# A hybrid decoder layer on one core: the output projection with the model's columns on the partitions, and x turned by VectorE block transposes through DRAM

## The chip, the core and the metric

The kernel runs on one core of a Trainium2 chip. A core has a matrix engine (TensorE, "PE" in the profile; its weight loads are "PEld"), a vector engine (VectorE, "DVE"), an activation engine (ScalarE, "ACT"), a general engine (GpSimd, "POOL") and a queue engine (SyncE, "SP") that here issues nearly all transfers to the sixteen DMA engines. SBUF is the working memory with 128 partitions, PSUM the small memory with eight banks into which TensorE writes, DRAM the large memory. The metric is the device time of one execution in microseconds (us); the kernel before took 1115.33 us, the median of three runs from 1115.24 to 1115.93.

## What is computed

One decoder layer for 1024 tokens of width 1024 (D), all in float32. The part that the change concerns, cut from the reference:

```python
        out_lru = rms_norm(h_lru * jax.nn.gelu(y_lru), lru_norm_w[l])       # 512 channels
        out_gdn = (rms_norm(o, gdn_norm_w[l]) * jax.nn.silu(z)).reshape(B, S, GDN_WIDTH)  # 512 channels
        mix = jnp.concatenate([out_lru, out_gdn], axis=-1) @ w_out[l]
        x = x + g1 * mix

        h = rms_norm(x, norm_mlp_w[l]) * (1.0 + sc2) + sh2
        x = x + g2 * (jnp.square(jax.nn.relu(h @ w_up[l])) @ w_down[l])

    return rms_norm(x, final_norm_w)
```

Ahead of it stand a norm of x, an input projection of 1024 by 3080, a gated linear recurrence (the LRU group) and a chunked gated delta rule with four heads (the GDN group). `g1`, `sc2`, `sh2` and `g2` are vectors over the 1024 columns of the model, worked out from `c` and `w_mod`.

## The kernel before, in words

**Precision.** Every large product is made of three matmuls on float32r operands: each operand is split into a rounded part "h" and a remainder "l", and h·h, h·l and l·h are summed (`mm3`). So a 128x128 by 128x512 step is three TensorE instructions, and each split costs a ScalarE cast and a VectorE or GpSimd subtraction.

**Order of the work.** The body does not issue instructions in program order. A recorder notes each operation with what it depends on, and `emit` then issues them in the order of a list of numbers that is stored in the kernel as packed text (`_ORDER`); a second list (`_SLOTS`) says which buffer each tile gets. So matmuls of several stages are interleaved one by one on TensorE, and each engine, SP among them, works through its own part of that list in order. The recorder is one line of code, which is why nearly every instruction of the profile has the line L331; stages are told apart by the names of the tiles.

**Input stages.** x (tiles of 128 tokens by 1024 columns) is normed and turned by TensorE, and the input projection gives channels on partitions and tokens along the free dimension. `key`, `query`, `value` and `chain` make the GDN group (output tiles `zz`, stored to `cat_d`), `lru` makes the LRU group (stored to `lru_d`), and `msum` gathers the squares of the LRU channels for their norm. The block transpose helper `blocks` (a VectorE transpose of 32x32 blocks over a tile of 128x1024) and its DRAM round trip are already used for the keys and values.

**Output projection.** `catload` loads the two groups back (tiles `gcm`, `lcm`) and splits them for the halves of 512 tokens (`gch`, `gcl`, `lch`, `lcl`); `wout` loads a row block of `w_out`, multiplies it by the norm weight and by g1 (broadcast over the partitions), and splits it. `gemm_o` then makes 128 tokens by 512 columns in one PSUM bank: the activations are stationary, the weights moving, twelve matmuls. There are sixteen such groups for the GDN channels (tiles `wg`), each added by VectorE to the tile of x that was loaded from DRAM, and sixteen for the LRU channels (tiles `wl`), each multiplied by the reciprocal norm `rsl` of its token and added. The tokens stand on the partitions, so `rsl` is a scalar per partition, and g1 has to be in the weights.

**Second norm.** For each of the eight token tiles `norm2` squares x with a sum along the row (ScalarE), takes the power of minus one half on GpSimd (`rsqrt8`), scales the row, stores the tile of x to DRAM (`x1_d`), and turns the eight 128x128 blocks on TensorE (tiles `h2T`); ScalarE and VectorE apply the column's scale and shift while they move the blocks out of PSUM to `h2r`. Three of the four quarters of the result are split at once (`h2h`, `h2l`, in pieces of 128x256).

**MLP.** The up and down products use Strassen-like sums with seven products for two by two blocks; `sums2` makes the sums of the quarters, `up` consumes the products in the order 1, 2, 6, 5, 7, 4, 3 (tiles `upx`, `upy`, `upz`). Products 1 and 2 need only the first half of the tokens, product 6 needs the sums over both halves. Four of the sixteen column blocks can be begun with products 1 and 2 before the first sum is there. The down product (tiles `dn`) goes over seven products again, and during the second of them the tiles of x are loaded back from `x1_d` (tiles `xb`); then the gated result is added and the final norm is made (`final_early`, `final_late`, `final_parts`).

Of the kernel before, what the change touches and what calls it, by code (L numbers as in the profile page):

```python
# [106 lines left out]
def dram_box(ap):  # L107
# [8 lines left out]
    'c-obl2Xqxx_xAUhB!m!p$IwxF2~E0!2+~17M4E-B2nYyBQ;JCMVxft^OO=kIAc&wy?@d}H^e#O>GH3sPXObYk-}n93`qo{^ojZ5t%szWR``OPvGq<3mlKmPcMI<HfMZ'  # L116
    '}Y%T8zI^a!`xPF@2~JeD|jsc~Q1#4!O*qkxTlFw36|9N9)N}t;$~o*{N0J500xW+cb-$mNS}3Zfa&}DPL$;M%<*&bM`s@mzOU&Zcxa&gxy-6(H?Lm)w5bgzSbEsKwp<'
    '#nnF%%3)!waw33vPax#<eFX_87jjQ<Vb(VCJBYH{;NH|u9Vs9zQ%dxBVu9lE!IixXqQ1dZ<8o9@uvh#nhrj)93LI326XBnkAXP(s)l1~T8#~hPKu4{rG)mrkG=9O6eQ'
    '99^ttt(444OUw1qV1)Y?8c_QnVBb7bdJ8rjJN7@eDd{#wv}=En*7GG4dkKT(nZo*3(G$BBuq+UeY9ki&3Lu1Y+^R07_Y2E$rufhdYqqKGRQ=IReI`FiIkt2n<s9jX{4'
    '_#)>mY#=9l!$C>H;vkk&F)N6A;(NEWDS2R$gO_`WOAS<2^jI*XWglMnI1MIFhp&fc8(HH8ddv}ffpR<6~Lbt&_XlodqgfR@r%%@VG3j89vLZx*@1c{SyGb^fcwEY@jF'  # L120
    '@NipuOMk7;wQg%kyft4Zm_yb@zKle0y{j52g^0#d{8=0vgyDmV`k1X8+CKD~_+Mp^Wc5~>!U_90f45%Ktg;8|i_1@Z-s3g$*XT|C!WcPWQ%jVIwafHFbJ9k#{a8P@9Y'
    'D-Iouq^1nvT;CBrU!fCWG*41m65uK4Yu~(o*-DT{f!>*DvH2K3he!?tt<;cyzXw!}nilC6gO3G?f2ng^&=x1ekiPKS(bPm(em%$ID0fE+aEvMW$rOw$G)i?g&ZgXJP('
    'FiDLmG+E{B7xm(QnsJ<_~Lmxk$2@dN^7Wssc>+5K~O)C~3HqbZaWw{Tg@-bFjvTBfiFa5a2T>VCufq|V|d8GCrR`v1qN!{l4@#~TiS2QCLy9K&Z%M1DoqlHR09l)_;I'
    'o5a^{323Gx--jy(o9C_%b@aO8I705f`L(7M;Un#d*VRb0%^e~)rHu;T3RvZWgtpHX1KV&-DG15(5HNpQeM+2nM{V2_O|(zc(+6=mz>f(*p*VwGtbHzuRr6fBcQ7|OcH'
    '{v9#}ZQRZGjWdRit(TJ1>gcjo_oZKFpdH<nxn7bn!$4a~S3h<jNlNL~F&_Ud^oJEZsdt}54GDof-)cCfUQO!}LAFAa60-j-(C9hRsjzv>lY-A3Br*FW@;z9bc~;1BkH'
    'rW=S*W1T2(a^^%bGl6f%zzx&LzINU@zouN2)wUCJSf~fIttmksEwZ06_wkIp(l#^i>$_UTys5+W8{)M=Kf$~4T2E(7BfPyD9Hcirw6!cFHdW-2PSN^0N#>C=F9zI{QZ'
    'C32+XlaGx3Sv7c*LSIe%mZ3$kNd;-Ze?bD@;pz%k6Xew#g?CY^3*t9Rya}$b9`8&t}ti%wSz++Su#*7M%PU*Dj2$H*9(Nz^Hb^_YcX<N~RW;4w3FQlc^&u%?JJu-YOd'
# [12 lines left out]
    'I4V4|@hOm{QJ^Jar}8M@j=o57~OzsdU&HY=bj?PEB4ye_qez4a*AZ20aqQ&#%h_T~!pK9!W$Q|Q>&;WHbkg|yPr-{tktaWc*}Fn4v3U&k!91w&HHo`mIIDrxSo^kUF='  # L140
    'o~h!0?oHDI+6i|1TkEs`8S!)|UBnFgrin2<wYlHP3?gRXa>r|Dm)c_934ek|{qn<QwO8NI8M0Xm`{Nkph#v+rc9`mRBe^<WS6KyBZ<tO}+x~3E=|{5Ll(jG0T;6&AYp'
# [247 lines left out]
def hybrid_body(ctx, tc, x, c, norm_mix_w, norm_mlp_w, w_mod, b_mod, w_in,  # L389
# [837 lines left out]
    def lru(ct, st, yy):  # L1227
# [509 lines left out]
```

## Time and profile before

| | |
|---|---|
| median of three runs | 1115.33 us |
| the profiled execution's own time | 1115.21 us |
| its span, first to last instruction | 1113.4 us |
| TensorE busy | 1102.6 us (99%) |
| VectorE busy | 784.2 us (70%) |
| ScalarE busy | 614.6 us (55%) |
| GpSimd busy | 246.0 us (22%) |
| DMA traffic | 240.30 MB in 132520 packets |

The page gives for each engine the time in which it had an instruction in flight. TensorE's instructions overlap: one matmul of 512 columns is shown with about 0.39 us, but the next one starts some 0.23 us after it, so the share says that it always had something to do and not how fast. The groups of instructions are listed as engine, operation, the tile written and the tiles read, their shape, a count, the busy time and the mean time of one. The view of a stretch of time gives for each engine its busy time there and, in brackets, how many instructions it touched, then the granted TensorE clock, the DMA engines' share and the transfer rate.

### The profile page before, as it was taken

The page shows a single profiled execution, that of the slowest core. Times are in us where ns is not written, and L with a number is a line of the kernel's source. Part 1 is how long each engine was busy: PE and PEld are TensorE (multiplying, and loading weights), DVE is VectorE, ACT ScalarE, POOL GpSimd, SP SyncE. Part 2 cuts the span into 40 slices and gives each one's busy share as a digit, 9 for nine tenths or more (in the row PEclk, how much of TensorE's full clock was granted, in tenths as well). Part 3 has the DMA queues.
Part 4 walks back from the last instruction along what each step waited for, and adds up shares of the span by engine and source line. Part 5 has one row for each costly group of instructions (what it writes and reads, how often), then busy time and mean ns, then how long its engine had stood idle before and what let it go on. Part 6 is the DMA issues. An engine that isn't in the chain of part 4 may idle for free.

```text
span 1113.4 us, 16336 instructions
## 1 busy us (share of the span) xinstructions
PE 1102.6 (99%) x6186; PEld 920.5 (83%) x6186; DVE 784.2 (70%) x1119; ACT 614.6 (55%) x956; POOL 246.0 (22%) x159
## 2 busy tenths in 40 slices
PE   9999999999999999999999999999999999999997
PEld 8799888888887878788888888788888888888886
DVE  5779996878787774798666757767574576673564
ACT  6759454536388882876645545455555433442442
POOL 1000200110204324000113121222500466903130
PEclk9999999999999999999999999999999999999999
DMA  9837815566751741310787687678999866946312
GB/s 342 305 111 248 287 62 176 191 226 214 263 170 69 254 161 50 138 53 29 256 288 247 234 293 252 220 235 292 380 376 397 326 230 222 341 171 245 132 57 94
DMA packets 132520, 240.30 MB, mean 216 GB/s; under 512 B 11141, under 2 KB 55770, under 8 KB 132442
## 3 DMA queue, kind: packets, MB, share of 16 engines
q1 hardware_dynamic: 132202, 239.04, 61.4%
q8 instruction: 48, 0.79, 0.3%
q14 instruction: 30, 0.25, 0.1%
q10 hardware_dynamic: 240, 0.23, 0.1%
HBM read 178.38 MB, written 60.86 MB: 215 GB/s over the span
## 4 chain that ended last, share of the span: by engine, by line
PE 91%; ACT 5%; DVE 2%; issue 1%; POOL 0%; POOLq 0%; ACTq 0%
PE dn L331 28%; PE upx L331 16%; PE upz L331 8%; PE k_p L331 4%; PE wg L331 4%; PE upy L331 4%; PE wl L331 4%; PE ly_p L331 4%; PE v_p L331 3%; PE q_p L331 3%; PE lx_p L331 3%; PE ch L331 2%; PE z_p L331 2%; PE cho L331 1%; ACT L331 1%
## 5 line engine op out<-in xcount | busy, mean ns | idle before, releaser
L331 PE MATMUL upx<-h2h,U 128*128 128x512 f32 x512 | 164.9, 395 | 0.0
L331 PEld LDWEIGHTS upx<-h2h,U 128*128 128x128 f32 x512 | 96.1, 188 | 22.8 <-ACT ek L331 0.7
L331 DVE TENSOR_TENSOR U<-wu,U 128x512 fp32r<-128x512 f32 x112 | 82.0, 751 | 23.8 <-ACT U L331 22.9
L331 POOL TENSOR_TENSOR wd<-wd,wd 128x512 f32<-128x512 f32 x32 | 45.6, 1429 | 238.4 <-DMA wd<-in_w_down_dram 181.8
L331 PE MATMUL upx<-h2l,U 128*128 128x512 f32 x256 | 95.2, 396 | 0.0
L331 ACT ACTIVATE act<-act 128x512 f32<-128x512 f32 x112 | 68.9, 629 | 32.7 <-DVE act L331 31.4
L331 ACT CAST U<-wu 128x512 fp32r<-128x512 f32 x112 | 66.6, 616 | 36.6 <-DVE wu L331 24.0
L331 PE MATMUL upz<-h2h,U 128*128 128x512 f32 x256 | 86.6, 394 | 0.0
L331 PEld LDWEIGHTS upx<-h2l,U 128*128 128x128 f32 x256 | 48.1, 188 | 11.5 <-issue 0.4
L331 PEld LDWEIGHTS upz<-h2h,U 128*128 128x128 f32 x256 | 48.1, 188 | 11.4 <-DVE act L331 0.2
L331 ACT COPY ek<-upx 128x512 f32<-128x512 f32 x48 | 27.7, 584 | 52.9 <-PE upx L331 52.5
L331 DVE TENSOR_TENSOR act<-upz,ek 128x512 f32<-128x512 f32 x32 | 22.0, 688 | 39.2 <-PE upz L331 20.0
L331 PE MATMUL upz<-h2l,U 128*128 128x512 f32 x128 | 47.9, 395 | 0.0
L331 PE MATMUL upy<-h2h,U 128*128 128x512 f32 x128 | 44.3, 398 | 0.0
L331 ACT ACT_TABLE_LOAD x28 | 35.9, 1283 | 11.7 <-DVE z_b L331 5.4
L331 POOL TENSOR_TENSOR R<-R,R_5o 128x1024 f32<-128x1024 f32 x8 | 22.9, 2872 | 81.8 <-DMA R_5o<-in_w_down_dram 81.8
L331 DVE TENSOR_TENSOR wu<-wu,wu 128x512 f32<-128x512 f32 x48 | 35.1, 736 | 0.4 <-DMA wu<-in_w_up_dram 0.2
L331 ACT ACTIVATE vn<-ch,bcoef 128x128 f32<-128x128 f32 x32 | 11.7, 367 | 34.2 <-PE ch L331 34.0
L331 PE MATMUL v_p<-hh,v_wh 128*128 128x258 f32 (+2 forms) x96 | 29.5, 335 | 0.9 <-ACT z_st L331 0.9
L331 PE MATMUL ly_p<-hh,ly_wh 128*128 128x512 f32 (+2 forms) x96 | 29.6, 326 | 0.3 <-ACT ta L331 0.3
L331 PE MATMUL v_p<-hl,v_wh 128*128 128x256 f32 (+2 forms) x96 | 29.8, 338 | 0.0
L331 PE MATMUL v_p<-hh,v_wl 128*128 128x258 f32 (+2 forms) x96 | 29.4, 335 | 0.0
(567 smaller groups left out, 3411.7 us busy)
## 6 DMA issues: line engine op xcount, KB each, us to landing
L<-aod SPq DMA_DIRECT2D x56, 512.0 KB
R<-in_w_down_dram SPq DMA_DIRECT2D x40, 512.0 KB
wu<-in_w_up_dram SPq DMA_DIRECT2D x32, 512.0 KB
aod<-as SPq DMA_DIRECT2D x64, 256.0 KB
wd<-in_w_down_dram SPq DMA_DIRECT2D x32, 512.0 KB
aod<-act SPq DMA_DIRECT2D x48, 256.0 KB
x<-in_x_dram SPq DMA_DIRECT2D x16, 512.0 KB
sc_w<-in_w_mod_dram SPq DMA_DIRECT2D x16, 512.0 KB
```

Source lines behind the costliest of these rows:

```text
L331: op.fn(*[res(v) for v in op.a], **{n: res(v) for n, v in op.k.items()})
```

## The change

The output projection now has the model's columns on the partitions and 512 tokens along the free dimension: the weights are stationary, the activations moving. The number of matmuls of the projection and their size stay. What goes with it:

- x is needed in the turned layout. `turn_x` loads each of the eight tiles of x again during the input projection, transposes its 32x32 blocks on VectorE and stores it to DRAM (`xb_d`); `residual` reads the turned tiles (`xT`) with runs of 64 floats.
- g1 is a scalar per partition now (`mod_col` instead of a row that is broadcast through DRAM), applied in `gated` while the result leaves PSUM; the weights get only the norm weight.
- The LRU norm can't be applied as a scalar per partition any more. `rows8` sums over the partitions by matmuls with ones, VectorE turns the sums, GpSimd takes the power, and the row goes through DRAM (`ln_d`) and comes back broadcast over the partitions (`lrus_b`); `catload` multiplies the LRU tiles by it before they are split.
- Four of the sixteen groups (`MERGED`, the second half of the tokens) sum the GDN and LRU channels in one PSUM bank, and leave PSUM once.
- The second norm is made for each half of the tokens after its eight column groups: squares and sums over the groups, `rows8`, and four TensorE transposes that spread the row over the partitions (`n2b`). There is no turn of the data itself. Scale and shift go over tiles of 128x512.
- x for the end is turned back: `turn_back` loads, block-transposes and stores the eight tiles during the up product, and `xload` reads them in two pieces each with runs of 64 floats. The operations of the final norm read x through strided views.
- `_ORDER` and `_SLOTS` are replaced, for the whole kernel.

The diff without the packed lists, cut to its core:

```diff
+    def turn_x(t):
+        xr, hb = big(f"xe{t}"), big(f"xeb{t}")
+        SP.dma_start(out=xr, in_=xs[t])
+        blocks(hb, xr)
+        SP.dma_start(out=xb_d[t], in_=hb)
...
+        if 6 <= i < 14:
+            turn_x(i - 6)
         if i == 7:
-            mod_row(2, 0, "g1")
+            g1 = mod_col(2, "g1")
...
-    V.tensor_scalar(two(rsl), colsum(msum, "lrus"), 1.0 / 512, 1e-6, op0=ALU.mult, op1=ALU.add)
-    rsqrt8(rsl, rsl)
+    def rows8(acc, name, n, scale):
+        pr, rw = ps(name), big(f"{name}_w")
+        mms([(pr[32 * j:32 * j + 32, 0:n], ones[:, 0:32], acc[:, n * j:n * j + n], True, True) for j in range(4)])
+        V.transpose(rw[:, 0:n], pr[:, 0:n])
+        r = small(f"{name}_r", n // 32)
+        V.tensor_scalar(r, rw[:, 0:n:32], scale, 1e-6, op0=ALU.mult, op1=ALU.add)
+        rsqrt8(r, r)
+        return r, rw
+    rl_, rw_ = rows8(msum, "lrus", 256, 1.0 / 512)
+    V.transpose(rw_[:, 256:512], bc(rl_, 32))
+    SP.dma_start(out=ln_d.rearrange("a (j n) -> (a j) n", j=4), in_=rw_[0:P:32, 256:512])
+    rlb = big("lrus_b")
+    SP.dma_start(out=rlb, in_=ln_d[0:1, :].to_broadcast([P, T]))
...
-        V.scalar_tensor_tensor(out=wr, in0=wr, scalar=sc, in1=g1b, op0=ALU.mult, op1=ALU.mult)
-        A.copy(wh, wr)
-        (V if k % 2 else G).tensor_tensor(out=wl, in0=wr, in1=wh.bitcast(F32), op=ALU.subtract)
+        A.activation(wh, wr, AF.Identity, scale=sc)
+        V.scalar_tensor_tensor(out=wl, in0=wr, scalar=sc, in1=wh.bitcast(F32), op0=ALU.mult, op1=ALU.subtract)
...
+    def gemm_o(p, cats, ws, k, hf, start, stop):
+        for q in range(4):
+            c, d = cats[(hf, q // 2)], slice((q % 2) * 512, (q % 2) * 512 + 512)
+            mm3(p, tuple(w[:, k * P:(k + 1) * P] for w in ws[q]), tuple(x_[:, d] for x_ in c), start and q == 0, stop and q == 3)
+    MERGED = ((1, 4), (1, 5), (1, 6), (1, 7))
+            SP.dma_start(out=v3(xT[q, hf], 64),
+                         in_=xb_d[4 * hf:4 * hf + 4].rearrange("t (i c) (b x) -> (c b) (t i) x", c=32, b=4)[:, :, 64 * q:64 * q + 64])
+    def gated(p, k, o, r):
+        V.scalar_tensor_tensor(out=v3(o, 32), in0=v3(p, 32), scalar=g1[:, k:k + 1], in1=r, op0=ALU.mult, op1=ALU.add)
...
+    def finish(k, hf):
+        p, o = ps(f"wl{k}{hf}"), slot(X1, k, hf)
+        if (hf, k) in MERGED:
+            gemm_o(p, gcat, gw_, k, hf, True, False)
+            gemm_o(p, lcat, lw, k, hf, False, True)
+            gated(p, k, o, residual(k, hf))
+        else:
+            gemm_o(p, lcat, lw, k, hf, True, True)
+            gated(p, k, o, v3(o, 32))
+        if k == 0:
+            norms[hf] = big(f"n2a{hf}")[:, 0:512]
+            A.activation(norms[hf], o, AF.Square)
+        else:
+            sq = half(f"n2s{k}{hf}")
+            A.activation(sq, o, AF.Square)
+            V.tensor_tensor(out=norms[hf], in0=norms[hf], in1=sq, op=ALU.add)
+    def norm2(hf):
+        r, _ = rows8(norms[hf], f"n2_{hf}", 128, 1.0 / D)
+        pb = ps(f"n2b{hf}")
+        for b in range(4):
+            tr(pb[:, b * P:(b + 1) * P], r[:, b:b + 1].to_broadcast([P, P]), ident)
+        rb = big(f"n2r{hf}")[:, 0:512]
+        V.tensor_copy(rb.rearrange("p (j b n) -> p j b n", j=4, b=4), pb.rearrange("p (b j n) -> p j b n", b=4, j=4))
+        for k in range(8):
+            rv = raw2[(g, hf)][e][:, d]
+            V.scalar_tensor_tensor(out=rv, in0=slot(X1, k, hf), scalar=A2[:, k:k + 1], in1=rb, op0=ALU.mult, op1=ALU.mult)
+            A.activation(rv, rv, AF.Identity, bias=sh2[:, k:k + 1])
+            if (g, hf) in alone:
+                A.copy(av, rv)
+                V.tensor_tensor(out=bv, in0=rv, in1=av.bitcast(F32), op=ALU.subtract)
-        for g in range(2):
-            ph = ps(f"h2T{t}_{g}")
-            for j in range(4):
-                tr(ph[:, j * P:(j + 1) * P], h2[:, (g * 4 + j) * P:(g * 4 + j + 1) * P], ident)
...
+    def turn_back(n):
+        SP.dma_start(out=xr, in_=x1_d[n])
+        blocks(hb, xr)
+        SP.dma_start(out=x1b_d[g, hf, e], in_=hb)
...
+    def xload(n):
+        th, tp, i = n // 4, n // 2 % 2, n % 2
+        b = x1[th, tp, i] = big(f"xb{n}")
+        for k in range(2):
+            SP.dma_start(out=b.rearrange("p (k q x) -> p k q x", k=2, q=8)[:, k],
+                         in_=x1b_d[i, th].rearrange("e (i c) (b x) -> (c b) (e i) x", c=32, b=4)[:, :, 128 * k + 64 * tp:128 * k + 64 * tp + 64])
```

More of the change, by code (lines that the diff above doesn't have):

```diff
@@ L1311, in catload @@
             SP.dma_start(out=m, in_=d_[h])
+            if norm is not None:
+                V.tensor_tensor(out=m, in0=m, in1=norm, op=ALU.mult)
             for hf in range(2):
@@ L1327, in hybrid_body @@
     gcat = catload("gc", cat_d)
     gw_ = [wout(k) for k in range(4, 8)]
-    def gemm_o(cats, ws, t, i, name, then):
-        p = ps(name)
-        s = halves[i]
-        hf, tt = t // 4, t % 4
-        for k in range(4):
-            ts_ = slice((k % 2) * 512 + tt * P, (k % 2) * 512 + (tt + 1) * P)
-            a, w = cats[(hf, k // 2)], ws[k]
-            mm3(p, (a[0][:, ts_], a[1][:, ts_]), (w[0][:, s], w[1][:, s]), k == 0, k == 3)
-        then(p, s)
-    x1 = [big(f"x1_{t}") for t in range(NT)]
@@ new lines, in hybrid_body, with residual @@
+    MERGED = ((1, 4), (1, 5), (1, 6), (1, 7))
+    X1 = {(g, hf): [big(f"x1_{g}{hf}{e}") for e in range(2)] for hf in range(2) for g in range(2)}
+    slot = lambda b, k, hf: b[(k // 4, hf)][k % 2][:, (k % 4 // 2) * 512:(k % 4 // 2) * 512 + 512]
+    xT = {}
+    def residual(k, hf):
+        q = k // 2
+        if (q, hf) not in xT:
+            xT[q, hf] = big(f"xT{q}{hf}")
+            SP.dma_start(out=v3(xT[q, hf], 64),
+                         in_=xb_d[4 * hf:4 * hf + 4].rearrange("t (i c) (b x) -> (c b) (t i) x", c=32, b=4)[:, :, 64 * q:64 * q + 64])
+        return v3(xT[q, hf], 64)[:, :, 32 * (k % 2):32 * (k % 2) + 32]
@@ L1349, in hybrid_body @@
+    def gated(p, k, o, r):
+        V.scalar_tensor_tensor(out=v3(o, 32), in0=v3(p, 32), scalar=g1[:, k:k + 1], in1=r, op0=ALU.mult, op1=ALU.add)
+    for hf in range(2):
+        for k in range(8):
+            if (hf, k) not in MERGED:
+                p = ps(f"wg{k}{hf}")
+                gemm_o(p, gcat, gw_, k, hf, True, True)
+                gated(p, k, slot(X1, k, hf), residual(k, hf))
+    lcat = catload("lc", lru_d, rlb)
     lw = [wout(k) for k in range(4)]
@@ L1414, in sums2 @@
         yield
-    for t in range(NT):
-        for i in range(2):
-            gemm_o(lcat, lw, t, i, f"wl{t}{i}",
-                   lambda p, s: V.scalar_tensor_tensor(out=x1[t][:, s], in0=p, scalar=rsl[:, t:t + 1], in1=x1[t][:, s],
-                                                       op0=ALU.mult, op1=ALU.add))
-        if t == 0:
-            dump("x1", x1[0])
-        norm2(t)
+    for hf in range(2):
+        for k in range(8):
+            finish(k, hf)
+        norm2(hf)
     wu_r = w_up.rearrange("a (k p) n -> (a p) k n", p=P)
@@ L1554, in hybrid_body @@
         if m < 10:
+            turn_back(m - 2)
             g2_acc = g2_acc or big("g2_acc")
@@ L1657, in add_to @@
     def add_to(th, i, j, v_, e):
-        e.tensor_tensor(out=xt(th, i, j), in0=xt(th, i, j), in1=v_, op=ALU.add)
+        e.tensor_tensor(out=xt(th, i, j), in0=xt(th, i, j), in1=v3(v_, 32), op=ALU.add)
     banks = {}
@@ L1668, in hybrid_body @@
             if at == 2:
-                x1[d] = big(f"xb{d}")
-                SP.dma_start(out=x1[d], in_=x1_d[d])
+                xload(d)
                 if d == 3:
```

322 lines of the change are left out of this document (153 added, 169 removed).

## The prediction

> **What bounds the kernel now.** I read the engines' shares first, then what TensorE waited for, then stretches of time. The shares and the chain that ended last:
>
> ```profile
> PE 1102.6 (99%) x6186; PEld 920.5 (83%) x6186; DVE 784.2 (70%) x1119; ACT 614.6 (55%) x956; POOL 246.0 (22%) x159
> PE 91%; ACT 5%; DVE 2%; issue 1%; POOL 0%; POOLq 0%; ACTq 0%
> ```
>
> TensorE always has a matmul in flight, and the chain goes through it for 91% of the span. All that it waited for (total, times, longest):
>
> ```profile
> PE warm L331 <- DVE ones L331: 1.0, 1, 1.0
> PE v_p L331 <- ACT z_st L331: 0.9, 1, 0.9
> PE gate L457 <- ACT ly_st L331: 0.7, 2, 0.4
> PE iy L457 <- ACT ttc L331: 0.5, 1, 0.5
> PE ly_p L331 <- ACT ta L331: 0.3, 1, 0.3
> ```
>
> Some 3.4 us in 1113. So the time is the number of TensorE instructions times their spacing, and a change is worth what it takes from that count, less the waits that it brings. The spacing comes from two stretches of 56 us, the first with the second norm's transposes, the other with none:
>
> ```profile
> 439.00:495.00 56.00, 56.00 (x276) 44.51 (x275) 45.81 (x102) 38.92 (x85) 4.23 (x7) 1.00 0.25 95
> 560.00:616.00 56.00, 56.00 (x243) 45.36 (x242) 36.54 (x55) 29.92 (x54) 12.51 (x9) 1.00 0.79 268
> L331 PE MATMUL h2T<-ident,h x64: 269/272/275, 439.7 to 492.4; 128*128 128x128 f32 x64
> ```
>
> The second gives 56/243 = 0.2305 us for a matmul of 512 columns. The first holds all 64 transposes and 276 - 64 = 212 matmuls; these take 48.9 us, which leaves 7.1 us, or 0.111 us for a transpose, though each is shown with 272 ns. The granted clock is 1.00 in both.
>
> **TensorE, part by part.** The projection's matmuls keep their number and size (16 + 16 groups of twelve), so the exchange of operands costs nothing here. The 64 transposes go: -7.1 us. New are two sums over partitions and eight transposes that spread the row:
>
> ```profile
> L457 PE MATMUL lrus_r<-msum,ones x8: 379/392/404, 416.4 to 416.6; 128*32 128x256 f32 x8
> 415.00:424.00 9.00, 0.64 (x8) 0.16 (x8) 0.37 (x1) 1.00 0.69 236
> L331 PE MATMUL lrus_c<-ident,lrus_row x2: 271/272/274, 418.2 to 418.6; 128*128 128x128 f32 x2
> ```
>
> The LRU sum of 256 columns takes 0.64 us (the second row is that tile alone). With 128 columns it is between half of that and the whole; I take half, since the columns are what streams: 2 x 0.32 = 0.6 us, at most 1.3. The eight transposes are 8 x 0.111 = 0.9 us. The LRU norm loses its two transposes and g1 gains two: nothing. Sum: -7.1 + 0.6 + 0.9 = -5.6 us, with bounds of -4.9 and, if the new ones all fell into gaps, -7.1.
>
> **Hand-over of the LRU norm.** Before, `rsl` was applied after the matmuls. Now the LRU operands can't be split before the norm has gone through DRAM and back. The GDN norm of each head already goes this way, and its rows give the first pass in order:
>
> ```profile
> L457 PE MATMUL on<-nv,ones x32: 378/379/404, 207.8 to 335.9; 128*32 128x256 f32 x32
> L331 SPq DMA_DIRECT2D on_b<-ond x4: 319/330/372, 215.8 to 343.2; - x4
> L331 DVE TENSOR_TENSOR zz<-zz,on_b x4: 1216/1216/1908, 220.8 to 358.6; 128x1024 f32<-128x1024 f32 x4
> L331 ACT CAST gch<-gcm x8: 602/614/623, 297.1 to 382.6; 128x512 fp32r<-128x512 f32 x8
> 417.00:445.00 28.00, 17.34 (x57) 10.53 (x57) 4.84 (x7) 1.00 0.16 57
> ```
>
> From the first sum (207.8) to the product with the broadcast row (220.8) are 13.0 us, then 1.2 us of it and 0.6 us of cast: 14.8 us at most, since that product may have queued on VectorE; up to the issue of the load at 215.8 alone it is 8.0 us, so 9.8 us is a lower bound. The cover is the last row, the GDN groups alone: 57 of their matmuls stand after the LRU sum at 416.4, 57 x 0.2305 = 13.1 us that need no LRU operand. The exposure is between nothing and 1.7 us.
>
> **Hand-over of the second norm.** For the first half of the tokens, its chain lies under the second half's projection: 8 x 12 matmuls, 22.1 us. For the second half the cover is products 1 and 2 of the four column blocks begun, 4 x 24 matmuls, again 22.1 us. The chain:
>
> ```profile
> L331 DVE SCALAR_TENSOR_TENSOR x<-wl,rsl,x 128x512 f32<-128x512 f32 x16 | 12.0, 748 | 10.4 <-PE wl L331 10.1
> L331 ACT ACTIVATE act<-act 128x512 f32<-128x512 f32 x112 | 68.9, 629 | 32.7 <-DVE act L331 31.4
> L331 DVE TENSOR_TENSOR x<-wg,x 128x512 f32<-128x512 f32 x16 | 10.8, 689 | 8.0 <-PE wg L331 8.0
> L331 DVE STREAM_TRANSPOSE on_w<-on x4: 409/444/450, 210.0 to 336.4; 128x256 f32<-128x256 f32 x4
> L331 POOL TENSOR_TENSOR ssq<-ssq,mhalf 128x1 f32<-128x1 f32 x16 | 11.4, 717 | 73.6 <-DVE ssq L331 73.4
> L331 ACT COPY ek<-upx 128x512 f32<-128x512 f32 x48 | 27.7, 584 | 52.9 <-PE upx L331 52.5
> L331 DVE TENSOR_TENSOR h2r<-h2r,h2r 128x1024 f32<-128x1024 f32 x8 | 9.8, 1222 | 0.1
> L331 DVE TENSOR_TENSOR h2l<-h2r,h2h 128x1024 fp32r<-128x1024 f32 x8 | 9.5, 1221 | 0.1
> 480.00:502.00 22.00, 22.00 (x106) 17.68 (x105) 20.61 (x36) 15.79 (x32) 0.55 (x1) 1.00 0.06 25
> 502.00:524.00 22.00, 22.00 (x96) 17.88 (x96) 21.13 (x28) 14.30 (x25) 0.00 (x0) 1.00 0.03 13
> ```
>
> Gating 0.75, square 0.63, add 0.69, the sum on TensorE 0.64, the turn 0.44, the power 0.72, four transposes 0.6 (0.27 and three more at 0.111), the copy at 0.58: 5.1 us. Then VectorE alone: eight scalings at 0.75, the four sums ahead of product 6 at 1.22 and two splits at 1.22, 13.3 us. Together 18.4 us against 22.1 us. VectorE also has four additions of about 0.69 us for the begun blocks in that time, and its share is 94% and 96% in these two stretches already, so 0.9 us is left: just covered if the 96 matmuls are kept for it. On ScalarE the shifts wait for VectorE here, and behind them are queued the copies `ek` that free PSUM banks for TensorE.
>
> I set down 0.5 us for each of the three hand-overs, the mean of the five waits of TensorE after the start (2.4 us): +1.5 us. Their bounds are nothing and the prices of the rivals.
>
> **VectorE, ScalarE, GpSimd elsewhere.** Sixteen block transposes are added, eight in the input projection and eight in the up product:
>
> ```profile
> L331 DVE STREAM_TRANSPOSE nv<-v2T 128x1024 f32<-128x1024 f32 x1 | 2.1, 2059 | 0.9 <-ACT v2T L331 0.9
> 83.00:300.00 217.00, 215.41 (x1852) 193.18 (x1851) 181.38 (x292) 121.42 (x199) 23.50 (x14) 1.00 0.61 205
> 560.00:720.00 160.00, 160.00 (x696) 128.88 (x695) 104.82 (x151) 81.19 (x145) 33.68 (x24) 1.00 0.75 254
> ```
>
> Eight times 2.06 us is 16.5 us. In the first stretch VectorE goes from 181.4 to 197.9 of 217 us, in the second from 104.8 to 121.3 of 160 us; it stays under TensorE in both, so the cost is nothing, and without that cover 16.5 us each. The page "VectorE: DVE Perf Modes" of the Trainium skill, "Rules for kernel authors", speaks against this: it gives the turn of a 128x128 tile to TensorE and keeps the vector engine for 32x32 blocks. By the rows above both sides are right: 33 us of VectorE replace 7.1 us of TensorE, and the rule would decide if VectorE did. The rest of VectorE's and ScalarE's work (fewer and larger pieces in the norm, four products with the LRU row at 1.22 us) changes by a few us and lies under TensorE as now. The strided views of the final norm have no row; between 0 and, at worst, double for the last pieces of 0.4 to 0.7 us, some 2 us; I take 0, since the counts of elements stay.
>
> **Transfers.** `turn_x` and `turn_back` each add 8 MB; the DMA engines' shares of 0.61 and 0.75 leave room for the 22 us that 8 MB take at 384 GB/s. x in both directions comes in runs of 256 B now, for which there is no row. The nearest are runs of about 500 B and the busiest stretch of long ones:
>
> ```profile
> DMA packets 3033, 1.50 MB, mean 300 GB/s; under 512 B 163, under 2 KB 3028, under 8 KB 3032
> 48.00:53.00 5.00, 5.00 (x37) 4.49 (x36) 4.93 (x5) 1.44 (x3) 0.00 (x0) 1.00 1.06 300
> 779.00:863.00 84.00, 84.00 (x364) 68.05 (x363) 50.81 (x49) 44.24 (x54) 14.34 (x10) 1.00 1.02 384
> L331 SPq DMA_DIRECT2D xb<-x1d x8: 320/333/599, 816.7 to 851.2; - x8
> L331 POOL TENSOR_TENSOR xb<-xb,keep x8: 1284/1750/2269, 885.2 to 1031.0; 128x512 f32<-128x512 f32 x8
> ```
>
> A packet of some 500 B takes 5 x 16 x 1.06 / 3033 = 0.028 us of one engine. A tile of 512 KB in runs of 256 B has 2048 packets: 1.4 us if only the bytes count (384 GB/s), 3.6 us if a packet costs as much as one of 500 B. Eight tiles add 0 to 18 us of DMA time, for the residual in a stage with room, for `xload` in the stretch from 779 to 863 us, where the DMA engines are full. I take nothing for the path: the tiles are needed 34 us after the last load (851.2 to 885.2). The Trainium skill ("DMA: Bandwidth & Descriptors", Specifications) says that transfers under 512 B miss the line rate because of a read-modify-write; by that the price would be at the upper end or above it.
>
> **The sum.** The profiled execution took 1115.2 us (span 1113.4 and 1.8 us around it): 1115.2 - 5.6 + 1.5 = 1111.1 us. It lies 0.1 us under the median, so the forecast is 1111.2 us.
>
> **The rivals.**
> - *VectorE becomes the bound at the second norm's barrier; slower.* Place: between the last projection matmul and product 6. For it: VectorE is full there now, and the scalings of four tiles, spread so far, fall into one burst behind a reduction. Against it: the bare chain is 3.7 us shorter than the cover. If half of the 96 matmuls are spent earlier, 11.1 us of cover are left for 18.4 us of chain and 2.8 us of additions: 10.1 us of stall, and 1115.3 - 5.6 + 10.1 + 1.0 = 1120.8 us. It decides from a stall of 7.8 us on, when some 38 matmuls are gone.
> - *The LRU row comes late; no change.* If the LRU group's own chain slips by 3 us because VectorE is fuller, the exposure is 1.7 + 3 us: 1115.3 - 5.6 + 4.7 + 1.0 = 1115.4 us.
> - *Short runs fill the DMA engines.* 18 us more of transfers in a full stretch; with half of it exposed as waits for the second product's operands, 1111.2 + 9 = 1120.2 us. Against it: the order can spread these loads over the 34 us.
> - *The transposes go and nothing is exposed*, and the 2.4 us of waits go too with the new order: 1115.3 - 5.6 - 2.4 = 1107.3 us.
> - *The change does not do what it says*: TensorE keeps eight transposes for the norm, which are in the sum; the data's own are all gone by the diff, so this gets no chance of its own.
>
> **How the numbers follow.** Forecast 0.53 (its own range 1108.6 to 1113.1), late LRU row 0.19, barrier 0.17, short runs 0.07, nothing exposed 0.04. The range reaches from the last case to the barrier's: 1107.5 to 1120. A run of this kernel tells 0.2% (2.2 us) from no change, so faster means below 1113.1: 0.51 of the forecast, the last case, and a little of the second, 0.58. Between 1113.1 and 1117.6 lie most of the second case and weak forms of the others: 0.20. Slower: 0.22.
>
> **What would show it.** No tile `h2T`, eight transposes `n2b`, and TensorE's busy time lower by 5 to 6 us: the sum is right. TensorE's waits should then hold `wl` on `lch` or `lcl`, and `upx` on `h2h` or `h2l`, each near 0.5 us; several us at `upx` with VectorE full before it is the barrier, several at `wl` the LRU row, and waits at `dn` behind a full DMA the short runs. Long waits in the input projection, with VectorE above 90%, would prove the block transposes not hidden, and the forecast wrong.

## The result, and the profile after

The changed kernel takes 1124.96 us, the median of six runs (1122.68 to 1125.85), the kernel before 1115.83 us beside it: a ratio of 1.0076, with a 95% interval from 1.0063 to 1.0089. It is slower by some 9 us where 4 us of gain were forecast, and outside the predicted range. Its profiled execution is the shortest of the six, 1122.68 us with a span of 1120.9 us.

The engines' shares, the chain that ended last and the packets, from the page of the changed kernel:

```profile
DMA packets 167785, 256.96 MB, mean 229 GB/s; under 512 B 44485, under 2 KB 88986, under 8 KB 167706
PE 1099.6 (98%) x6146; PEld 916.6 (82%) x6146; DVE 822.6 (73%) x1116; ACT 603.4 (54%) x919; POOL 228.2 (20%) x149
PE 56%; ACT 4%; DVE 4%; DMA 2%; issue 2%; POOL 1%; POOLq 0%; SPq 0%; DVEq 0%; ACTq 0%
```

TensorE's busy time is lower by 3.0 us, and the chain goes through it for 56% of the span instead of 91%. What it waited for, in total, times and longest (the nine largest):

```profile
PE wl L333 <- ACT lch L333: 3.5, 1, 3.5
PE wg L333 <- DVE x L333: 2.2, 1, 2.2
PE dn L333 <- DVE R_5l L333: 2.1, 1, 2.1
PE n2b L333 <- POOL n_r L333: 1.6, 2, 0.9
PE ch L333 <- DVE nv L333: 1.5, 1, 1.5
PE warm L333 <- DVE ones L333: 1.0, 1, 1.0
PE iw L459 <- ACT LT L333: 1.0, 1, 1.0
PE gate L459 <- ACT ly_st L333: 0.7, 1, 0.7
PE lrus L459 <- POOL msum L333: 0.6, 1, 0.6
```

The waits of before were 1 us or less each and 3.4 us together. Seven of these rows are new (`warm` and `gate` were there before). Only the first and the fourth belong to the hand-overs that the prediction had in its sum. It had named `dn` as the place where a full DMA would show, but VectorE ends this wait; and it had named waits in the input projection, as `ch` and `iw` are, as the sign that the block transposes are not hidden. Between the first and the last matmul TensorE was idle for 13.6 us, before for 2.6 (gaps over 0.12 us): 11.0 us more.

A second loss is in no list of waits. Three stretches around the wait at `iw`, with TensorE's busy time first and the granted clock third from the right:

```profile
166.40:170.80 4.40, 3.42 (x120) 3.15 (x120) 4.29 (x7) 3.13 (x6) 0.00 (x0) 0.96 0.38 143
170.80:173.60 2.80, 2.80 (x25) 1.89 (x19) 2.77 (x4) 1.94 (x4) 0.00 (x0) 0.50 1.03 365
173.60:178.00 4.40, 4.40 (x78) 3.90 (x76) 2.19 (x4) 1.66 (x3) 0.16 (x1) 0.97 1.07 369
```

The wait of 1.0 us ends at 169.1 us; 1.3 us later the clock falls to one half and stays there for 3.4 us (170.4 to 173.8 in slices of 0.2 us), so TensorE, though busy, does half its work: 1.7 us lost. The six runs show a mean clock from 0.998 (the profiled one) to 0.992, and the longest of them has the lowest clock; so more of such stretches are the likely cause of the 2.3 us between the profiled run and the median. Those runs left no profile, but kernels edited from this one show one to four stretches in theirs, as told below.

Between the two profiled runs the last matmul ends 7.7 us later, at 1114.4 us instead of 1106.7. Idle time is 11.0 us of that and half clock 1.7 us; so -5.0 us are left for the work that is gone, where the prediction had -5.6. This is a remainder; what a transpose costs is measured at the end of the experiments.

### The profile page after: what moved, and what is told of

It reads as the page before. It is cut to its first block, busy times and chain, and to the rows that moved or that the text cites. A ratio compares the mean times of both kernels' runs of the same rounds, so it can differ in the third digit from the quotient of the medians.

```text
span 1120.9 us, 16319 instructions
## 1 busy us (share of the span) xinstructions
PE 1099.6 (98%) x6146; PEld 916.6 (82%) x6146; DVE 822.6 (73%) x1116; ACT 603.4 (54%) x919; POOL 228.2 (20%) x149
## 4 chain that ended last, share of the span: by engine, by line
PE 56%; ACT 4%; DVE 4%; DMA 2%; issue 2%; POOL 1%; POOLq 0%; SPq 0%; DVEq 0%; ACTq 0%
PE dn L333 25%; PE upx L333 15%; PE upz L333 8%; PE wl L333 4%; PE upy L333 4%; DMA L<-aod 1%; ACT ta L333 1%; DVE xr L333 1%; ACT L333 1%; POOL R L333 1%; ACT ti L333 1%; DMA lrus_b<-lnd 1%; DVE as L333 0%; DMA lrud<-ly_st 0%; DVE U L333 0%
## 5 line engine op out<-in xcount | busy, mean ns | idle before, releaser
L333 PE MATMUL upx<-h2l,U 128*128 128x512 f32 x256 | 91.1, 394 | 0.0
L333 PE MATMUL upz<-h2h,U 128*128 128x512 f32 x256 | 90.2, 396 | 0.2 <-DVE act L333 0.2
L333 PE MATMUL q_p<-hh,q_wh 128*128 128x512 f32 (+2 forms) x96 | 30.1, 335 | 0.0
L333 PE MATMUL q_p<-hl,q_wh 128*128 128x512 f32 (+2 forms) x96 | 29.9, 336 | 0.0
L333 PE MATMUL v_p<-hh,v_wl 128*128 128x256 f32 (+2 forms) x96 | 29.6, 333 | 0.0
L333 PE MATMUL v_p<-hh,v_wh 128*128 128x512 f32 (+2 forms) x96 | 29.4, 333 | 0.0
```

The source lines that it names most:

```text
L333: op.fn(*[res(v) for v in op.a], **{n: res(v) for n, v in op.k.items()})
```

## The experiments

**What the LRU row costs, and whether turn_x is hidden.** In both edits `rec.mute` marks operations that keep their number in the written order and are not issued.

```diff
+    rec.mute = True
     V.transpose(rw_[:, 256:512], bc(rl_, 32))
     SP.dma_start(out=ln_d..., in_=rw_[0:P:32, 256:512])
     SP.dma_start(out=rlb, in_=ln_d[0:1, :].to_broadcast([P, T]))
+    rec.mute = False
...   (and the four products with norm in catload)
```

> The changed kernel without the LRU row's way back: the second transpose, the store, the broadcast load and the four products with the row are left out, so the LRU norm is summed and raised to its power but not applied. Against the kernel before at 1115.8 us and the changed one at 1125.0 us. Theory (the LRU hand-over costs the 3.5 us that TensorE waited at wl for lch, and the queue behind it a little more): 1121.5 us or up to 1 us less, ratio 1.005, and no wait of wl above 0.5 us. Rival (the operands of the LRU groups are late anyway, because their loads and casts stand behind the residual's loads on SP and behind VectorE): at least 2 us of the wait stay, 1123.5 to 1125 us, ratio 1.007 to 1.008.

Measured: 1120.99 us, ratio 1.0049 [1.0033, 1.0065], 4.0 us below the changed kernel, and no wait at `wl`. The theory holds. The other waits of the list stood as before, but for the small one at the sum itself (`lrus`), which is gone; three are new in this profile, `lx_p` with 1.2 us, `upz` with 0.8 and `xTp` with 0.7. The first comes 150 us before the work that was left out, behind the late load of a weight; the same wait stands with 0.8 to 1.2 us in the profiles of six of the kernels here and with less than 0.2 us in the others. In the changed kernel the row's way is this (VectorE's, SP's and GpSimd's rows):

```profile
413.62 0.45 DVE L333 STREAM_TRANSPOSE lrus_w<-lrus 128x256 f32<-128x256 f32 x1 [2.24 <-PE lrus L459]
...
417.04 0.45 DVE L333 STREAM_TRANSPOSE lrus_w<-lrus_r 128x256 f32<-128x256 f32 x1 [1.54 <-POOL lrus_r L333]
...
426.12 2.36 DVE L333 TENSOR_TENSOR lcm<-lcm,lrus_b 128x1024 f32<-128x1024 f32 x2 [3.97 <-DMA lrus_b<-lnd]
```

```profile
419.17 0.32 SPq L333 DMA_DIRECT2D lrus_b<-lnd  x1
```

```profile
L333 POOL TENSOR_TENSOR lrus_r<-lrus_r,mhalf 128x8 f32<-128x8 f32 x1 | 2.7, 2652 | 1.6 <-DMA lrud<-ly_st 1.6
```

The power took 2.65 us while VectorE split weights beside it. A power of the same shape took 1.65 us in the kernel before, where it was the LRU norm's too:

```profile
L331 POOL TENSOR_TENSOR rsl<-rsl,mhalf 128x8 f32<-128x8 f32 x1 | 1.6, 1648 | 0.3 <-DVE rsl L331 0.3
```

It took 1.65 us again in the two last versions below, whose order keeps the splits away from it, so 1.0 us came with the splits. (The 0.72 us in the prediction is the power of a tile with one column.) The broadcast load needed 7 us from its issue to the product. From the sum at 412.8 us to the end of the first cast at 428.1 us are 15.3 us, and the matmuls that need no LRU operand lasted 11.3 us of them:

```profile
413.30:424.70 11.40, 11.32 (x51) 8.75 (x47) 6.79 (x10) 0.00 (x0) 2.65 (x1) 1.00 0.44 122
424.70:428.10 3.40, 0.00 (x0) 0.00 (x0) 1.98 (x2) 0.65 (x2) 0.00 (x0) 1.00 1.08 373
```

The second edit leaves `turn_x` out and lets the residual read `xs` in its place with the same access pattern.

> The changed kernel without turn_x (eight loads, eight block transposes and eight stores of the input projection are left out); the residual reads x itself with the same runs of 256 B, so x is added unturned. Theory (the block transposes on VectorE and their transfers cost the waits iw 1.0 and ch 1.5 us in the input projection): 1122.5 us, ratio 1.006, and both waits gone or under 0.3 us each. If the dip of the granted clock at 170 to 180 us of the span also came from them, 1.7 us more: 1120.8 us, ratio 1.0045. Rival (the block transposes are hidden, as the prediction took them; the two waits come from the order of VectorE's other work): 1124.5 to 1125.5 us, ratio 1.008.

Measured: 1125.68 us, 1.0089 [1.0073, 1.0105], no gain at all. The rival holds: the block transposes and their 8 MB are hidden, as the prediction had it. The waits that I had laid to them are all still there:

```profile
PE ch L337 <- DVE nv L337: 1.5, 1, 1.5
...
PE iw L463 <- ACT LT L337: 1.0, 1, 1.0
```

So they do not come from `turn_x`; that they come from where other work stands in the order, which was written anew for the whole kernel, is tried further below.

**The price of the transposes, in the kernel before.**

```diff
+            j0 = min(range(4), key=lambda j: ORDER.index(len(rec.ops) + j))
             for j in range(4):
+                rec.mute = j != j0
                 tr(ph[:, j * P:(j + 1) * P], h2[...], ident)
...   (the four readers of the bank read block j0)
```

> The kernel before with 48 of its 64 transposes of the second norm left out: of each four that share a bank only one is issued, and all four readers read its 128 columns (so the normed operand is wrong in three quarters of its places); nothing else moves. Price as the prediction took it (0.111 us a transpose): 1115.8 - 5.3 = 1110.5 us, ratio 0.995, TensorE's busy time down by 5 us. Rival (the transposes partly fill gaps, or VectorE and ScalarE set the time there): 1113 us or more, ratio above 0.9975, with new waits of TensorE at upx or h2T.

Measured: 1113.20 us, 0.9979 [0.9969, 0.9989]: 2.6 us for 48 transposes, half of the price: the rival holds. The page and the waits say where the other half went:

```profile
PE 1098.0 (99%) x6138; PEld 914.3 (82%) x6138; DVE 787.1 (71%) x1119; ACT 614.8 (55%) x956; POOL 246.8 (22%) x159
```

```profile
PE h2T L335 <- ACT h L335: 0.9, 1, 0.9
PE h2T L335 <- ACT h2h L335: 0.8, 1, 0.8
```

TensorE's busy time fell by 4.6 us, and its idle time rose by 2.6 us, 1.8 of them at the transposes that were left, where ScalarE's part of the norm now ends the wait. So the price on TensorE was about right, and the cover around it was thinner than one sees from TensorE's side.

**Four causes at once.** Besides the two edits above, `turn_back` is muted and `xload` reads `x1_d` in runs of 2 KB, and the n2b transposes read a constant:

```diff
-            tr(pb[:, b * P:(b + 1) * P], r[:, b:b + 1].to_broadcast([P, P]), ident)
+            tr(pb[:, b * P:(b + 1) * P], ones, ident)
```

> The changed kernel with four edits: the LRU row's way back left out (as in e_lru_row), turn_x left out (as in e_no_turn_x), the block transposes and the transfers of turn_back left out with the end reading the unturned sums in runs of 2 KB, and the eight n2b transposes reading a constant tile instead of the second norm's row, which is left out. Theory (the waits explain the loss): 3.5 (LRU row), 2.5 (iw and ch), 2.1 (dn), 1.6 (n2b), with 0 to 1.7 us of the clock's dip: 1125.0 - 9.7 = 1115.3 us, down to 1113.6 us; the wait at wg of 2.2 us stays. Rival (the loss lies in the spacing of the matmuls or in the count, and waits that go come back elsewhere): above 1118 us, ratio above 1.002.

Measured: 1116.57 us, 1.0007 [0.9998, 1.0017], 8.4 us below the changed kernel, between the theory and its rival. Of the waits that the theory let go, `wl` and `n2b` are gone; `iw` and `ch` stayed, as in the run without `turn_x`, and against the expectation the 2.1 us at `dn` stayed too, although `turn_back`'s work was gone. Between the two profiled runs 6.1 us are gained: idle time is lower by 5.4 us, and there are two stretches at half clock instead of one. So waits are the greater part of what was gained, but not all of it; some 2 us stay open.

**What made R_5l late.** VectorE's timeline in the changed kernel at that place, start and duration first:

```profile
960.04 3.40 DVE L333 TENSOR_TENSOR R_5l<-R,R_5h 128x1024 fp32r<-128x1024 f32 x1 [9.63 <-POOL R L333]
963.36 3.42 DVE L333 TENSOR_TENSOR L_7l<-L,L_7h 128x1024 fp32r<-128x1024 f32 x1
966.71 3.40 DVE L333 TENSOR_TENSOR R_5l<-R,R_5h 128x1024 fp32r<-128x1024 f32 x1
```

The same subtraction takes 1.22 us elsewhere. GpSimd ran its own subtractions (`R<-R,R_7o`) without a break meanwhile, also at 3.4 us instead of 2.4 us.

```diff
+            rec.mute = at == 7
             G.tensor_tensor(out=m, in0=m, in1=o, op=ALU.subtract)
+            rec.mute = False
```

> The changed kernel with GpSimd's eight subtractions for the seventh product's right operands left out (these operands are then not the differences). Theory (VectorE's splits of R_5l and its neighbours took 3.4 us each because GpSimd worked beside them, and 1.2 us otherwise; this made R6_5l late): the splits between 957 and 972 us take 1.2 us, the 2.1 us wait of dn goes, 1122.5 us. Rival (the splits are slow for another reason, and the wait stays): 1125 us with 3.4 us splits.

Measured: 1121.50 us, 1.0046 [1.0028, 1.0064], from two runs 2 us apart; the wait at `dn` is gone, and VectorE's rows read:

```profile
960.05 1.23 DVE L337 TENSOR_TENSOR R_5l<-R,R_5h 128x1024 fp32r<-128x1024 f32 x1 [7.37 <-DMA R_7o<-in_w_down_dram]
961.19 1.22 DVE L337 TENSOR_TENSOR L_7l<-L,L_7h 128x1024 fp32r<-128x1024 f32 x1
```

So the split is slow because of GpSimd's work: one pair of instructions needs 3.4 us, about 1.2 + 2.4, as if the two engines took turns. The Trainium skill ("SBUF — State Buffer", Who interferes with whom) says that such a VectorE instruction contends with GpSimd's reads; these rows agree.

**The short runs.** Both turned reads are made long:

```diff
-  in_=xb_d[4 * hf:4 * hf + 4].rearrange("t (i c) (b x) -> (c b) (t i) x", c=32, b=4)[:, :, 64 * q:64 * q + 64]
+  in_=v3(xb_d[4 * hf + q], 64)
-  in_=x1b_d[i, th].rearrange("e (i c) (b x) -> (c b) (e i) x", c=32, b=4)[:, :, 128 * k + 64 * tp:128 * k + 64 * tp + 64]
+  in_=x1b_d[i, th, tp][:, 512 * k:512 * k + 512].rearrange("p (q x) -> p q x", q=8)
```

> The changed kernel with both turned reads in long runs: the residual's tiles are read in rows of 4 KB and the end's tiles in runs of 2 KB, at the same places of the order and with the same bytes (so x and the sums stand in the wrong places). Theory (the runs of 256 B cost transfer time that lies under TensorE): 1124 to 1125.5 us, ratio 1.0075 as the changed kernel. Rival (they cost time on the path: the gated groups wait for xT behind the LRU loads, and the second product's operands for the end's loads): wg's 2.2 and dn's 2.1 us go, 1120.5 us, ratio 1.004.

Measured: 1124.76 us, 1.0081 [1.0061, 1.0101], the same as the changed kernel, with 2.2 us at `wg` and 2.1 us at `dn` as before. The rival falls: the runs of 256 B are off the path.

**What a wait costs.** Sixteen waits were made in the up product of the kernel before. A matmul that adds to a bank is moved directly behind the copy that reads this bank, and the copy is made two, three or four times:

```diff
-        A.copy(ek[:, hi_], px)
+        hold(n, 6, ek[:, hi_], px)      # TIMES copies in 16 places, one elsewhere
```

> The kernel before, its whole computation, with 16 made waits of TensorE in the up product: in 16 places the next accumulating matmul of a bank stands directly behind the copy that reads this bank, and the copy is made twice, so TensorE waits some 1.3 us each time in a stretch where it waited for nothing. Theory A (a wait costs itself): 1115.8 + 16 x 1.3 to 1.45 = 1137 to 1139 us, ratio 1.02, granted clock 1.00 throughout. Theory B (a wait of this length is followed by some 3.4 us at half clock, as behind iw in the changed kernel, so another 1.7 us): 1115.8 + 16 x 3.1 = 1165 us, ratio 1.045, with 16 stretches at 0.5. Between the two: the count of such stretches times 1.7 us should make up the difference from theory A.

> As the kernels with 16 made waits of 1.3 us (0 stretches at half clock, 1.62 us each in all) and 2.5 us (11 of 16 places with a stretch), the copy made three times: some 1.85 us each. If a stretch follows only from a length between the two on: none, 1115.8 + 16 x 2.2 = 1151 us. If the chance rises evenly from 1.3 us: five or six stretches of 1.7 us, 1160 us.

> As the run with 16 made waits, the copy made four times, so TensorE waits some 2.45 us in each of the 16 places. Theory A (a wait costs itself): 1115.8 + 16 x 2.5 = 1156 us, ratio 1.036, granted clock 1.00. Theory B (each is followed by 3.4 us at half clock): 1156 + 16 x 1.7 = 1183 us, ratio 1.06. If the chance of such a stretch rises with the length of the wait, more of the 16 places show it than in the run with 1.3 us.

The waits came out as meant. First with two copies, then with four:

```profile
PE upx L325 <- ACT ek L1469: 20.7, 16, 1.3
```

```profile
PE upx L325 <- ACT ek L1469: 40.4, 16, 2.5
```

The stretch that holds them all, with two, three and four copies (TensorE's busy time first, granted clock third from the right):

```profile
520.00:800.00 280.00, 259.32 (x1106) 204.56 (x1106) 173.45 (x251) 149.20 (x263) 51.21 (x36) 1.00 0.67 227
```

```profile
520.00:800.00 280.00, 249.47 (x997) 195.63 (x996) 156.13 (x226) 142.57 (x252) 44.02 (x32) 0.94 0.59 198
```

```profile
520.00:800.00 280.00, 239.55 (x948) 187.45 (x947) 147.27 (x216) 145.00 (x256) 41.84 (x30) 0.93 0.57 191
```

| waits of TensorE | time | above before | stretches at half clock |
|---|---|---|---|
| 16 x 1.3 us | 1141.87 us, 1.0234 [1.0219, 1.0249] | 26.0 us | 0 |
| 16 x 1.9 us | 1169.14 us, 1.0473 [1.0454, 1.0492] | 53.0 us | 10 |
| 16 x 2.5 us | 1177.99 us, 1.0561 [1.0545, 1.0576] | 62.1 us | 11 |

Neither theory was right alone. A wait of 1.3 us costs 1.62 us, so 0.3 us more than the list shows, and no clock. From 1.9 us on ten or eleven of sixteen are followed by a stretch at half clock, each of 3.4 us (in slices of 0.2 us), which begins 0 to 1.3 us after the wait's end: 30.5 us of waits, 16 x 0.3 and ten times 1.7 us make 52.3 of the 53.0 us. For 2.5 us the same sum gives 63.9 us, where 62.1 were measured. In these places the chance does not rise evenly; it steps up between 1.3 and 1.9 us.

Elsewhere the length alone does not decide. The changed kernel and the five kernels above that were edited from it, with its order, share most of their waits; in their six profiles stretches at half clock followed so:

| wait | length | profiles that have it | followed by a stretch |
|---|---|---|---|
| `iw` | 0.9 to 1.0 us | 6 | 4 |
| `ch` | 1.5 us | 6 | 0 |
| `wg` | 2.2 us | 6 | 5 |
| `wl` | 2.6 to 3.5 us | 4 | 3 |
| `dn` | 2.1 us | 5 | 1 |

The kernel without `turn_x` has four of them in its profiled run of 1127.1 us. Three of them, in slices of 5 us (granted clock third from the right):

```profile
170.00:175.00 5.00, 5.00 (x94) 3.96 (x92) 3.75 (x6) 2.55 (x5) 0.00 (x0) 0.66 0.91 329
...
405.00:410.00 5.00, 5.00 (x16) 3.93 (x16) 4.96 (x5) 1.30 (x3) 0.00 (x0) 0.66 0.10 18
...
430.00:435.00 5.00, 5.00 (x17) 3.92 (x16) 4.31 (x5) 2.26 (x5) 4.21 (x3) 0.66 0.28 106
```

The run with waits of 1.9 us also has an eleventh stretch outside the sixteen places, at 172 us, 2 us after a wait of 0.5 us that the kernel before has too, there without a stretch. What decides beside the length stays open. The Trainium skill ("TensorE: Matmul & The Clock Gate", Why this matters for your kernels) asks for no idle gaps over some 3 us; here 1.9 us was enough in ten of sixteen places, and the measurement decides.

**Taking the waits away without leaving work out.** What the order does is seen at `wg`. Its matmuls need a PSUM bank that VectorE's gating (`x<-wg`) frees, and in the changed kernel this gating stood in VectorE's queue behind the clamp of the LRU block (`ta<-ta`):

```profile
400.37 2.75 DVE L333 TENSOR_SCALAR ta<-ta 128x1024 f32<-128x1024 f32 x1
403.04 1.40 DVE L333 SCALAR_TENSOR_TENSOR x<-wg,g,xT 128x512 f32<-128x512 f32 x2
```

The wait ended at 403.8 us, with the first of these two gatings. First five places of the order alone: GDN gating of two groups ahead of the LRU block's clamp on VectorE, `nv` ahead of the eighth g1 product, `R6_5l` ahead of `L0_7l`, and on TensorE a few ready matmuls ahead of `iw` and of the n2b transposes.

> The changed kernel with the moves in the order alone (gating of two groups, nv, R6_5l, iw, n2b); the LRU row still goes through DRAM. Theory (each wait belongs to its place): iw 1.0, nv 1.5, dn 2.1 and n2b 1.6 us go, the 2.2 us of wg come back at the LRU sum or at wl, since the row's way back still ends at the same time: 1125.0 - 6.2 = 1118.8 us, ratio 1.0027, and down to 1116.5 us if stretches at half clock go with the waits. Rival (all 8.4 us go): 1116.5 us with the dips kept. Rival (the waits return): above 1122 us.

Measured: 1119.55 us, 1.0032 [1.0021, 1.0043], within 0.8 us of the theory and 5.4 us below the changed kernel, by the order alone. The waits on `nv` and `R_5l` and those at `n2b` are gone, and `iw` is down to 0.3 us. In one point the theory was wrong: 2.0 us are still waited at `wg`, at a later group, and did not move to the LRU sum or to `wl`, which has its 3.3 us as before. In the next kernel the row is also spread by TensorE, in the bank of its own sum (in short; each group of four transposes is one operation of the recorder):

```diff
-    V.transpose(rw_[:, 256:512], bc(rl_, 32))
-    SP.dma_start(out=ln_d..., in_=rw_[0:P:32, 256:512])
-    SP.dma_start(out=rlb, in_=ln_d[0:1, :].to_broadcast([P, T]))
+    for b0 in (0, 4):
+        for b in range(4):
+            tr(pr_[:, b * P:(b + 1) * P], rl_[:, b0 + b:b0 + b + 1].to_broadcast([P, P]), ident)
+        A.copy(rlb...[:, :, b0:b0 + 4, :], pr_.rearrange("p (b j n) -> p j b n", b=4, j=4))
```

> The changed kernel with its whole computation, two edits. (1) The LRU row is spread by eight TensorE transposes into the bank of its own sum and two ScalarE copies, in place of the transpose, the store and the broadcast load through DRAM. (2) Five places of the written order: GDN gating of two groups ahead of the LRU block's clamp on VectorE, the split of wo1 and wo2 behind the power of the LRU row, nv ahead of the eighth g1 product, R6_5l ahead of L0_7l, and on TensorE five or so ready matmuls ahead of iw, of the n2b transposes and of the LRU sum. Theory (the loss is these hand-overs, 3.5 + 2.2 + 2.1 + 1.6 + 1.5 + 1.0 = 11.9 us of waits, and the 1.7 us stretches at half clock that follow some of them): 1125.0 - 11.9 + 0.9 for the eight transposes = 1114 us with the dips kept, 1110.5 to 1112.5 us with most of the dips gone; ratio 0.995 to 0.9985. Rival (the waits come back elsewhere because VectorE is too full): 1117 us or more.

Measured: 1116.46 us, 1.0007 [0.9997, 1.0016]; 8.5 us gained, 2.5 us less than expected with the dips kept. The list shows why:

```profile
PE wg L327 <- DVE x L327: 2.1, 1, 2.1
...
PE upy L327 <- DVE U L327: 0.9, 1, 0.9
```

The waits at `wl`, `dn` and `n2b` are gone, and no stretch at half clock is left in its profile. The wait at `wg` had only gone to a later group whose gating is queued on VectorE behind the LRU block. The two versions that follow take the waits in the list of the one before in the same way, by moves in the order.

> The changed kernel with its whole computation: as the version with the row by TensorE and the moved order (v1), with further moves: the gating of wg50 ahead of the LRU block's product on VectorE (v1 still waited 2.1 us at wg for it), the power of the LRU row with VectorE kept off the splits of wo1 and wo2, and on TensorE one to four ready matmuls ahead of the second gate, of two steps of the GDN chain, of the second norm's sum and of upy2. Theory (each wait goes with its place, and costs 0.3 us more than it shows, as the made waits did): v1's 1116.5 less 2.1 + 0.9 + 0.7 us and three times 0.3 us = 1112 us, ratio 0.9965 against the kernel before. Rival (the wait moves on to wl, whose LRU operands come no earlier): 1114.5 to 1116 us, ratio 0.9985 to 1.000.

Measured: 1115.61 us, 0.9991 [0.9982, 1.0000]. The rival holds: 1.3 us stand at `wl` now, and 1.1 at `upz`. The 1.0 us at `lx_p` are the late load that comes and goes between runs.

> The changed kernel with its whole computation: v2 with its last waits of TensorE (lx_p 1.0, wg 0.6, wl 1.0 and 0.3, n2b 0.4, upz 0.9 us) met by the order alone: one to six ready matmuls ahead of each, and one cast of a weight ahead of two activations on ScalarE. Theory (the sparing of TensorE, 5.6 less 0.9 us for the row's transposes, is there and was eaten by the waits, each of which costs 0.3 us more than it shows): v2's 1115.6 less 4.2 and 5 x 0.3 us = 1110 us, ratio 0.9945 to 0.9965. Rival (VectorE or ScalarE is now what sets the time, and the waits come back at other tiles): 1114 us or more, ratio above 0.998.

Measured: 1113.82 us, 0.9978 [0.9969, 0.9987]: faster than both kernels, though close to what the rival said. Its page and its waits:

```profile
PE 1100.1 (99%) x6154; PEld 916.6 (82%) x6154; DVE 818.2 (74%) x1115; ACT 604.6 (54%) x921; POOL 226.6 (20%) x149
```

```profile
PE warm L327 <- DVE ones L327: 1.0, 1, 1.0
PE wg L327 <- ACT ta L327: 0.9, 1, 0.9
PE wl L327 <- ACT lch L327: 0.8, 1, 0.8
PE upy L327 <- DVE n2r L327: 0.6, 1, 0.6
```

Some 1.6 us of idle time are left above that of the kernel before (4.2 against 2.6 us), in eleven gaps against six. With 0.3 us for each of the five more: -5.6 + 0.9 + 1.6 + 1.5 = -1.6 us. Measured are -2.2 us between the medians and -1.3 us between the two profiled runs.

Into this kernel 48 transposes are put back (in short):

```diff
-            tr(pb[:, b * P:(b + 1) * P], r[:, b:b + 1].to_broadcast([P, P]), ident)
+            for _ in range(1 if hf else 13):
+                tr(pb[:, b * P:(b + 1) * P], r[:, b:b + 1].to_broadcast([P, P]), ident)
```

> v3 with 48 transposes put back: each of the four n2b transposes of the first half of the tokens is issued thirteen times, to the same place. By the price that the prediction used (0.111 us a transpose in the stream) 48 x 0.111 = 5.3 us above v3. Rival (a transpose in the stream is cheaper, as the 2.6 us for 48 of them in the kernel before suggested): 2 to 3 us above v3. If the bank or the second norm's chain, which ends later by the same time, makes TensorE wait, the trace shows that wait behind n2b, and it is taken off.

Measured: 1119.07 us, 1.0028 [1.0018, 1.0038], 5.25 us above v3, with the same waits but for 0.1 us:

```profile
PE 1105.0 (99%) x6202; PEld 920.9 (82%) x6202; DVE 816.7 (73%) x1115; ACT 604.5 (54%) x921; POOL 226.9 (20%) x149
```

That is 0.109 us for a transpose where TensorE sets the time; the prediction had 0.111.

## Why the prediction was wrong, step by step

- **TensorE's count, -5.6 us: right.** A transpose in the stream costs 0.109 us where TensorE sets the time, and in the changed kernel's profile the remainder is -5.0 us, or -6.5 us if each of the five more gaps costs 0.3 us beside its length. No `h2T` is left, and n2b has eight transposes, as said. The price of the two sums was not measured alone. The sign that I named for the count, a busy time lower by 5 to 6 us, was not there (3.0 us): a stretch at half clock alone makes the busy time 1.7 us longer.
- **The LRU row, 0.5 us: wrong, and the first failing step.** The prediction set a chain of 9.8 to 14.8 us against a cover of 13.1 us, and took 0.5 us from an exposure of 0 to 1.7. Measured were 15.3 us of chain and 11.3 us of matmuls. The cover had been counted in the old order. The lower bound of the chain let the load land at once, and it took 7 us; the power took 1.0 us more beside VectorE's splits. The wait was 3.5 us, and leaving the row's way out gave 4.0 us. The rival "the LRU row comes late" had the right place and, with 4.7 us, about the size; its reason, the LRU group's own chain slipping by 3 us, is not what is seen (TensorE waited 0.6 us at the sum), and it held everything else at its forecast.
- **The second norm, two times 0.5 us: nearly right.** The two waits at n2b are 1.6 us together. They end with the power, which took 1.4 us each for its tile of four columns, where the sum had the 0.72 us of a tile with one. No wait came behind them in the changed kernel: the 96 matmuls were a cover, and the barrier rival, the slower case with the most weight, did not happen.
- **All else as before: wrong, and the larger error.** Four waits of 6.8 us (`wg` 2.2, `dn` 2.1, `ch` 1.5, `iw` 1.0) stand where the sum had no term. In the input projection and the down product the diff changes no matmul, but the order list is new from end to end, and each engine's queue with it; moving five places of that list, n2b's among them, gave 5.4 us with no other edit. `wg` is a queue effect of the kind that I had asked about at the second norm only: gating that frees a bank stood on VectorE behind the LRU block's chain. `dn` was a split that took three times as long beside GpSimd and stood late in VectorE's queue; leaving out GpSimd's work and moving the split ahead each took the wait away.
- **The clock: not in the sum.** The row of before with 1.00 was read as a property of the kernel, while it held for a TensorE with hardly a gap. Most of the waits of 2 us and more, and some of 1 us, brought a stretch that costs 1.7 us on top.
- **Block transposes, strided views, short runs, 0 us: right as far as tried.** Without `turn_x`, and with long runs, the time stays the same, though packets under 512 B rose from 11141 to 44485. `turn_back`'s transposes were left out only together with three other things, and the strided views were not tried alone.

The sum with the measured terms, for the profiled runs: 56 transposes at 0.109 us less the two sums at the 0.3 us of the prediction are -5.5 us, so 1115.2 - 5.5 + 11.0 + 1.5 (five more gaps) + 1.7 = 1123.9 us, against 1122.7 measured; 1.2 us stay open. With the order mended and the row spread by TensorE the change is worth 2.2 us (v3), half of what was forecast; the other half would need a version without any of its new waits, which was not reached.

## What to carry to other kernels

When an order that was written for the whole program is made anew, a forecast needs a term for every stage, not only for those whose work changes: look at each queue for the instruction that frees a bank or an operand and ask what stands ahead of it. Price a step of a chain from a row of the same shape, and with what runs beside it: a power took 0.55 us with one column and 1.65 us with eight, and 2.65 us with VectorE's splits beside it; a split of 1.2 us took 3.4 us beside GpSimd. On a TensorE that is busy without a gap, a wait cost more here than its length: 0.3 us each, and 1.7 us more where a stretch at half clock followed, which was so for ten of sixteen waits of 1.9 us and for none of sixteen of 1.3 us, but also for some of 1 us.

## What the runs showed of the hardware

- After a made wait of TensorE of 1.9 us the granted clock fell to one half in 10 of 16 places, after 2.5 us in 11 of 16, after 1.3 us in none. Each stretch lasted 3.4 us and began 0 to 1.3 us after the wait's end, some 2 to 4 us after its beginning. In six profiles with the changed kernel's order a wait of 1.0 us was followed by one in four, a wait of 1.5 us in none.
- Sixteen waits of 1.3 us in a dense stream, with the clock at 1.00, cost 1.62 us each.
- A VectorE subtraction of two tiles of 128x1024 in SBUF took 1.22 us alone and 3.4 us beside a GpSimd subtraction of the same shape, which itself went from 2.4 to 3.4 us.
- A power on GpSimd took 0.55 us for 128x1, 1.4 us for 128x4 and 1.65 us for 128x8.
- A transpose of 128x128 in float32, shown with 272 ns, took 0.109 us of the stream, measured by adding 48 of them.
